# Two transformer blocks on one core: the gate's dense steps moved into the HGRN stage, and half the stick-breaking heads' values multiplied as whole float32 numbers

## The chip, the cores and the metric

The kernel runs on one core of a Trainium2 chip. The metric is device time in microseconds (us) for one launch, the median of three runs. The profile is one more execution, taken with the hardware profiler. Engines are named as in the profile: PE (matrix multiplies; PEld are its weight loads), DVE (vector), ACT (scalar and activation), POOL, and SP, which here only issues DMA transfers, in order.

## What is computed

Two blocks over 1024 tokens of width 1024, all in float32. Only the first block's mixing half is touched. There, one normed input `u` is multiplied by `w_in`, and the product is cut into four parts for HGRN (`hq`, `hf`, `hi` and the gate `hg`, 512 columns each) and three for stick-breaking attention (`sq`, `sk`, `sv`, 8 heads of 64):

```
o_hg = rmsnorm(hgrn2_mix(hq, hf, hi, lb)) * silu(hg)
z     = q.k * scale                              # causal, per head
rem   = cumsum_from_the_right(log(1 - sigmoid(z))) without its own term
a     = sigmoid(z) * exp(rem)
o_sb  = a @ v                                    # then rmsnorm
mix   = concat([o_hg, o_sb]) @ w_out
```

HGRN is a gated recurrence with 4 heads of 128. What follows (output projection, feed-forward, the whole second block) is the same in both kernels.

## The kernel before, in words

**Dense products.** A float32 product is made of rounded parts: every operand is split into a high part and a rest (`split`, line 215: a cast at L218, a subtraction at L224), and `mm3` (L300 to L302) issues three single-pass matmuls, high times high, high times rest, rest times high. A weight unit is 1024 columns by 128 rows of `w_in`. `a_steps` takes one unit for 128 output columns (48 matmuls), `b_steps` four units for 512 columns (8 steps of 24 matmuls). `Weights` loads units in the order in which `register` lists them, two raw loads and four split units at a time. Below, "dense matmul" always means one of L300 to L302.

**HGRN stage** (`mix1`). Each HGRN head is a chain of 12 steps (`hgrn_steps`): `diag`, seven levels `lev` (matmuls at L746, and on DVE and POOL the updates on which the next level depends), `kt`, `ds` and two `out`. `merge` deals these steps out among the dense steps of the list `main`.

**Stick-breaking stage** (`sb`). For a head and each of 8 strips of 128 queries, `score` multiplies q by k (L968, L969, a mask at L971), takes two sigmoids (ACT, L972, L973), a running product from the right (DVE, L975) and a product (DVE, L977). `pv_steps` then goes by pairs of strips: PE transposes the weights (L869), ACT copies them out as a high part (L872), DVE makes the rest (L873), and four matmuls of 256 or 128 columns multiply them by `vs`, which holds high and rest of v side by side in 128 columns (L882, L886, L888). The two halves are added at the end (ACT copy L892, DVE add L983). `after_pair` transposes and squares what two heads gave (L992, L996) and stores it to `osbT`. Ten such groups make a head.

The dense steps that `mix1` returns (`rest`) are dealt out among these steps. `load` of a head pair waits, by the third entry of its step, until the dense steps of that pair's q and k were recorded: q and k go through DRAM (store `ev_T`, L687; load L836, L839).

**The order.** A scheduler orders the recorded steps; stick-breaking steps have a priority 300 ahead of the dense ones (`AHEAD`). The order on each engine is then fixed when the kernel is built, and each engine works in that order.

**After it** `out1` multiplies by `w_out`, in two groups for each 128 tokens: one on the HGRN part, one on the stick-breaking part, which is read back from `osbT` (L1032).

Of the kernel before, what the change touches and what calls it, by code (L numbers as in the profile page):

```python
# [8 lines left out]
F32 = mybir.dt.float32  # L9
F32R = mybir.dt.float32r  # L10
# [8 lines left out]
P = 128  # L19
D = 1024  # L20
T = 1024
NT = T // P
# [174 lines left out]
class Kernel:  # L197
# [161 lines left out]
    def register(self):  # L359
        U = self.U = {}  # L360
        U["hi"] = self.b_units("w_in", 1024)
        pair = [("sq", 2048), ("sk", 2560)]
        for h in range(4):
            U["hq", h] = self.a_units("w_in", h * P, 1)
            U["hf", h] = self.a_units("w_in", 512 + h * P, 1)
            if h in (1, 2):

                U[pair[h - 1][0], 0] = self.a_units("w_in", pair[h - 1][1], 1)
        U["sv"] = self.b_units("w_in", 3072)
        for j in range(1, 4):  # L370
            for n, c0 in pair:
                U[n, j] = self.a_units("w_in", c0 + j * P, 1)
        U["hg"] = self.b_units("w_in", 1536)
        U["out"] = [self.b_units("w_out", c * 512, kind=("w", "xxxy")[c]) for c in range(2)]
        self.ffn_units(0, "w_gate_up", "w_gate_up", FF, "w_down", ("pg", "ple_gate", "ple_proj"))
        U["z0"] = self.b_units("w_in_2", 0, 416)
        U["dq"] = self.b_units("w_in_2", 416)
        U["dk"] = self.b_units("w_in_2", 928)
        U["dv"] = self.b_units("w_in_2", 1440)
        U["om"] = [self.b_units("w_out_2", c * 512, nk=4) for c in range(2)]  # L380
        U["od"] = [self.b_units("w_out_2", c * 512, k0=4, nk=4) for c in range(2)]
        self.ffn_units(1, "w_gate_2", "w_up_2", 0, "w_down_2", ("pg2", "w_ple_gate_2", "w_ple_proj_2"))
# [65 lines left out]
    def build(self):  # L448
        nc, A = self.nc, self.A
        self.constp = self.pool("const")  # L450
        self.smallp = self.pool("small", 4)
        self.junkp = self.pool("junk", 1)
        self.W = Weights(self, RAWS)
        self.W.open_raw("raw", RAWS, self.ctx)
        self.W.open("w", 4, self.ctx)
        self.psp = self.pool("psum", 1, space=PSUM)
        dram = self.pool("scratch", 1, space=DRAM)
        dt = lambda name, shape: dram.tile(shape, F32, tag=name, name=name)
        self.S = {n: dt(n, s) for n, s in dict(
            hgg=[T, 512], ohg=[T, 512], osbT=[512, T], h1=[T, D], h2=[T, D],  # L460
            rm=[4, 2, T], dv=[T, 512], omT=[512, T], od=[T, 512], h3=[T, D], act=[FF, T], bias8=[4, 1152], skew=[4, P * 1152]).items()}
        for n, sh in dict(qk=[96, 16, 2, T], vm=[T, 8, P], sq=[8, P, T], sk=[8, P, T], sv=[T, 8, P], dq=[8, P, T], dk=[8, P, T]).items():
            self.S[n] = dram.tile(sh, F32, tag=n, name=n)

        self.register()
        self.constants()
        self.block1()
# [175 lines left out]
    def mix1(self):  # L643
        nc, S, U = self.nc, self.S, self.U
        st = nc.sync.dma_start
        with ExitStack() as c:
# [41 lines left out]
                return f  # L688

            def ev_sv(ps, i):  # L690
                t = tmp.tile([P, 8, 2, 64], F32R, tag="hl", name="stage")
                self.split(t[:, :, 0, :], t[:, :, 1, :], ps.rearrange("p (h d) -> p h d", h=8), "act", "dve")
                st(out=S["sv"][i * P:(i + 1) * P], in_=t.rearrange("p h a d -> p h (a d)").bitcast(F32))

            def ev_gate(ps, i):
                s = tmp.tile([P, 512], F32, tag="s", name="sg")
# [4 lines left out]
            def head(h):  # L701
                return self.a_steps(U["hq", h][0], ev_q(h)) + self.a_steps(U["hf", h][0], ev_f(h))

            def pair(j):
                return (self.a_steps(U["sq", j][0], ev_T(S["sq"], j))
                        + self.a_steps(U["sk", j][0], ev_T(S["sk"], j)))

            first = head(0)
            p0 = pair(0)
            main = head(1) + p0[:8] + head(2) + p0[8:] + head(3) + self.b_steps(U["sv"], self.u_of, ev_sv) + pair(1)  # L710
            side = []
            for h in range(4):
                side += self.hgrn_steps(h, H[h])
            self.run(first + side[0:2])
            self.merge(side[2:], main, AHEAD["hg"], BY["hg"])
        return pair(2) + pair(3) + self.b_steps(U["hg"], self.u_of, ev_gate)

    def hgrn_steps(self, h, X):
        nc, S = self.nc, self.S
# [130 lines left out]
        first = 384 if ext == 640 else min(512, ext)  # L850
        return [(0, first)] + ([(first, ext - first)] if ext > first else [])

    def pv_steps(self, X, h, put):

        nc = self.nc
        out = {}
        for I in range(NT // 2):
            L = []
            for jp in range(I + 1):
                def f(I=I, jp=jp):  # L860
                    ps = self.ps("tr")
                    a0, a1 = X["a", 2 * I], X["a", 2 * I + 1]
                    j0, j1 = 2 * jp, 2 * jp + 1
                    if jp < I:
                        blocks = [(a0, j0), (a1, j0), (a0, j1), (a1, j1)]
                    else:
                        blocks = [(a0, j0), (a1, j0), (a1, j1)]
                    for n, (a, j) in enumerate(blocks):
                        nc.tensor.transpose(ps[:, n * P:(n + 1) * P], a[:, j * P:(j + 1) * P], self.ident)  # L869
                    w = len(blocks) * P  # L870
                    at = self.atp.tile([P, 2, 512], F32R, tag="at", name="at")
                    nc.scalar.copy(at[:, 0, 0:w], ps[:, 0:w])  # L872
                    nc.vector.tensor_tensor(at[:, 1, 0:w], ps[:, 0:w], at[:, 0, 0:w].bitcast(F32), ALU.subtract)  # L873
                    X["at", I, jp] = at

                def g(I=I, jp=jp):
                    if jp == 0:
                        X["pv"] = self.ps("pv")
                    pv, at, vs = X["pv"], X.pop(("at", I, jp)), X["v"]
                    j0, j1 = 2 * jp, 2 * jp + 1  # L880
                    for hl in range(2):
                        nc.tensor.matmul(pv[:, 0:256], vs[:, j0, :], at[:, hl, 0:256],  # L882
                                         start=jp == 0 and hl == 0, stop=False)
# [11 lines left out]
            out[I] = L  # L895
        return out

    def attention_steps(self, heads, load, score, make_put, after_pair, order, need=lambda h: 0):

        steps = []  # L900
        queue = []
# [11 lines left out]
        steps.append((0.1, prep(0)))  # L913
        prev = []
        for h in range(heads):
            L = self.pv_steps(X[h], h, make_put(X))
            left = list(range(NT // 2))
            for n, i in enumerate(order):
                if n == 2 and h + 1 < heads:
# [19 lines left out]
    def sb(self, rest):  # L939
        nc, S, U, A = self.nc, self.S, self.U, self.A  # L940
        self.banks = {"d": [0, 1], "z": [2, 3, 4], "tr": [5, 6], "pv": [7]}
        with ExitStack() as c:
# [8 lines left out]

            def load(h, X):
                X[h]["q"], X[h]["k"] = self.load_stack(S["sq"][h], S["sk"][h])
                X[h]["v"] = self.load_v(S["sv"], h)
                if h % 2 == 0:
                    X[h]["o"] = X[h + 1]["o"] = op.tile([P, T], F32, tag="o", name="sb_o")

# [22 lines left out]
            def make_put(X):  # L980
                def put(h, I, pv, t):
                    r = (h % 2) * 64
                    nc.vector.tensor_tensor(X[h]["o"][r:r + 64, I * 256:(I + 1) * 256], pv[0:64, 0:256], t, ALU.add)  # L983
                return put

# [12 lines left out]
                nc.scalar.activation(o, o, AF.Copy, scale=self.cols[:, COL_SB + j:COL_SB + j + 1])  # L998
                nc.sync.dma_start(out=S["osbT"][j * P:(j + 1) * P, :], in_=o)

            side = self.attention_steps(8, load, score, make_put, after_pair, ORDER["sb"], lambda h: max(0, h // 2 - 1) * 16)
            self.merge(side, rest, AHEAD["sb"], BY["sb"])


# [971 lines left out]
```

## Time and profile before

| | |
|---|---|
| runs | 2895.56, 2894.29, 2891.99 us; median 2894.29 |
| profiled execution | 2897.28 us, of which the span of its instructions is 2895.5 us |
| PE busy | 2777.6 us, 96% of the span |
| DVE busy | 1756.3 us, 61% |
| ACT busy | 1163.4 us, 40% |
| POOL busy | 712.3 us, 25% |
| granted PE clock | 0.991 of full speed on the mean |

Busy times are unions: what overlaps is counted once, and a matmul counts until its last result is out, so that a PE that is busy all the time need not be at its peak. All stages of both blocks are in these shares; the stage of interest lies between 62 and 600 us. Windows below are us from the start of the span.

### The profile page before, as it was taken

What the parts mean: (1) busy time and instruction counts of PE and PEld (TensorE: products, weight loads), DVE (VectorE), ACT (ScalarE), POOL (GpSimd) and SP (SyncE); (2) the same over time, 40 slices, a digit from 0 to 9 for tenths busy, and PEclk for the clock granted to TensorE, in tenths of its full rate; (3) what the DMA queues carried; (4) which work ended last, traced back from release to release, by engine and by line L of the source; (5) the groups of instructions that cost most, each with busy time, mean ns of one, the idle gap of its engine ahead of it and who ended that gap; (6) DMA issues with size and microseconds to landing.
All of it is one profiled execution on the core that took longest, in us unless ns stands there. A gap on an engine that the chain in (4) does not pass through costs nothing. (4 is left out here: it accounts for less than half of the span.)

```text
span 2895.5 us, 37271 instructions
## 1 busy us (share of the span) xinstructions
PE 2777.6 (96%) x13699; PEld 2281.7 (79%) x13699; DVE 1756.3 (61%) x3132; ACT 1163.4 (40%) x2237; POOL 712.3 (25%) x608
## 2 busy tenths in 40 slices
PE   8989998988999999999999999989999999999999
PEld 6878767776888888887788788767778888788887
DVE  4444598768444334667478775777875555556661
ACT  4211376745333334223246455656543333311131
POOL 1222100035433332223124000020243343222211
PEclk9989999999999999999999999999999999999999
DMA  4221645252322224332126855753422222343211
GB/s 134 73 71 65 175 124 135 93 183 73 95 87 84 83 78 165 102 104 91 65 102 178 217 151 175 203 131 76 139 73 81 80 88 87 118 166 104 77 65 46
DMA packets 277942, 321.36 MB, mean 111 GB/s; under 512 B 14646, under 2 KB 207194, under 8 KB 276222
## 3 DMA queue, kind: packets, MB, share of 16 engines
q1 hardware_dynamic: 277758, 318.97, 36.5%
q8 instruction: 108, 1.77, 0.3%
q14 instruction: 76, 0.62, 0.1%
HBM read 228.69 MB, written 92.59 MB: 111 GB/s over the span
## 5 line engine op out<-in xcount | busy, mean ns | idle before, releaser
L1249 PE MATMUL bank<-q,w 128*128 128x512 f32 x3696 | 846.6, 391 | 5.9 <-DVE q L1132 1.4
L1249 PEld LDWEIGHTS bank<-q,w 128*128 128x128 f32 x3696 | 693.3, 188 | 157.6 <-ACT s L1186 2.1
L218 ACT CAST w<-raw 128x1024 fp32r<-128x1024 f32 (+2 forms) x246 | 236.8, 971 | 495.9 <-DVE y L1315 185.9
L224 DVE TENSOR_TENSOR w<-raw,w 128x1024 fp32r<-128x1024 f32 (+2 forms) x242 | 311.7, 1297 | 128.1 <-ACT w L218 121.7
L1315 DVE TENSOR_TENSOR y<-y,bank 128x512 f32<-128x512 f32 x336 | 227.0, 686 | 162.1 <-PE bank L302 158.3
L300 PE MATMUL bank<-w,act 128*128 128x512 f32 x704 | 274.7, 390 | 2.7 <-DVE o L1231 2.7
L302 PE MATMUL bank<-w,act 128*128 128x512 f32 x704 | 274.7, 391 | 1.5 <-POOL act L224 1.5
L300 PE MATMUL bank<-w,u 128*128 128x512 f32 (+1 forms) x672 | 272.0, 405 | 3.1 <-DVE dn L1574 1.4
L301 PE MATMUL bank<-w,act 128*128 128x512 f32 x704 | 274.5, 390 | 0.0
L301 PE MATMUL bank<-w,u 128*128 128x512 f32 (+1 forms) x672 | 266.4, 396 | 3.3 <-POOL w L224 2.2
L302 PE MATMUL bank<-w,u 128*128 128x512 f32 (+1 forms) x672 | 265.9, 396 | 1.1 <-DVE u L296 1.1
L224 POOL TENSOR_TENSOR act<-act_raw,act 128x1024 fp32r<-128x1024 f32 x40 | 103.6, 2609 | 300.9 <-ACT act L218 300.9
L1186 ACT COPY s<-bank 128x512 f32<-128x512 f32 x132 | 77.4, 588 | 202.6 <-PE bank L1249 202.5
L300 PEld LDWEIGHTS bank<-w,act 128*128 128x128 f32 x704 | 132.6, 188 | 30.7 <-DVE o L1231 3.1
L302 PEld LDWEIGHTS bank<-w,act 128*128 128x128 f32 x704 | 132.5, 188 | 30.0 <-POOL act L224 2.2
L301 PEld LDWEIGHTS bank<-w,act 128*128 128x128 f32 x704 | 132.4, 188 | 27.2
L300 PEld LDWEIGHTS bank<-w,u 128*128 128x128 f32 x672 | 127.3, 189 | 26.6 <-ACT u L293 2.4
L301 PEld LDWEIGHTS bank<-w,u 128*128 128x128 f32 x672 | 127.2, 189 | 26.8 <-POOL w L224 3.1
L302 PEld LDWEIGHTS bank<-w,u 128*128 128x128 f32 x672 | 127.0, 189 | 26.2 <-DVE u L296 1.7
L224 DVE TENSOR_TENSOR w<-s,w 128x1024 fp32r<-128x1024 f32 x44 | 54.4, 1236 | 139.9 <-ACT w L218 139.9
L873 DVE TENSOR_TENSOR at<-bank,at 128x512 fp32r<-128x512 f32 (+1 forms) x160 | 99.8, 630 | 42.8 <-ACT at L872 41.6
L140 POOL TENSOR_TENSOR s<-raw 128x512 f32<-128x512 f32 x44 | 59.9, 1362 | 218.3 <-DVE w L224 137.4
(361 smaller groups left out, 5208.9 us busy)
## 6 DMA issues: line engine op xcount, KB each, us to landing
raw<-in_w_gate_up_dram SPq DMA_DIRECT2D x44, 512.0 KB
act<-o SPq DMA_DIRECT2D x88, 256.0 KB
raw<-in_w_down_dram SPq DMA_DIRECT2D x44, 512.0 KB
act_raw<-act SPq DMA_DIRECT2D x44, 512.0 KB
raw<-in_w_in_dram SPq DMA_DIRECT2D x40, 512.0 KB
qk<-qkT SPq DMA_DIRECT2D x32, 384.0 KB
raw<-in_w_gate_dram SPq DMA_DIRECT2D x22, 512.0 KB
raw<-in_w_up_dram SPq DMA_DIRECT2D x22, 512.0 KB
```

What stands on the lines that cost most here:

```text
L140: pool(x[:, HI], r2[:, LO], r2[:, HI], ALU.add)
L218: nc.scalar.copy(hi, src)
L224: e.tensor_tensor(lo, src, hi.bitcast(F32), ALU.subtract)
L300: mm(ps, lh, rh, start=start, stop=False)
L301: mm(ps, lh, rl, start=False, stop=False)
L302: mm(ps, ll, rh, start=False, stop=stop)
L873: nc.vector.tensor_tensor(at[:, 1, 0:w], ps[:, 0:w], at[:, 0, 0:w].bitcast(F32), ALU.subtract)
L1186: nc.scalar.copy(t, src)
L1249: nc.tensor.matmul(ps, w[:, a, o], (uh, ul)[b][:, k, :], start=bool(first) and n_mm == 0, stop=n_mm == 11, skip_group_check=True)
L1315: nc.vector.tensor_tensor(y, y, ps, ALU.add)
```

## The change

1. `register` and `mix1`: the gate's dense steps (`hg`, 8 steps of 24 matmuls) leave `rest` and become the last of the HGRN stage's `main`. In `main` the q and k products of stick-breaking pairs 0 and 1 now stand whole between the HGRN heads. `rest` keeps pairs 2 and 3.
2. Odd stick-breaking heads (1, 3, 5, 7): the weights are copied out of the transpose as whole float32 numbers, with no rest made on DVE. v is kept whole, 64 columns wide, in a DRAM tensor of its own (`sw`). Two float32 matmuls take the place of four single-pass ones; each is two instructions on PE. The result lies in 64 rows, and one ACT copy takes the place of a copy and a DVE add.
3. `ev_sv` splits only the even heads' half of v, and copies the odd half; it issues three stores for each 128 tokens where there was one.

```diff
         for h in range(4):
             U["hq", h] = self.a_units("w_in", h * P, 1)
             U["hf", h] = self.a_units("w_in", 512 + h * P, 1)
             if h in (1, 2):
 
-                U[pair[h - 1][0], 0] = self.a_units("w_in", pair[h - 1][1], 1)
+                pair_units(h - 1)
         U["sv"] = self.b_units("w_in", 3072)
-        for j in range(1, 4):
-            for n, c0 in pair:
-                U[n, j] = self.a_units("w_in", c0 + j * P, 1)
         U["hg"] = self.b_units("w_in", 1536)
+        pair_units(2)
+        pair_units(3)
...
             def ev_sv(ps, i):
-                t = tmp.tile([P, 8, 2, 64], F32R, tag="hl", name="stage")
-                self.split(t[:, :, 0, :], t[:, :, 1, :], ps.rearrange("p (h d) -> p h d", h=8), "act", "dve")
-                st(out=S["sv"][i * P:(i + 1) * P], in_=t.rearrange("p h a d -> p h (a d)").bitcast(F32))
+
+                t = tmp.tile([P, 3, 4, 64], F32R, tag="hl", name="stage")
+                v = ps.rearrange("p (h two d) -> p h two d", two=2, d=64)
+                w = t[:, 2].bitcast(F32)
+                self.split(t[:, 0], t[:, 1], v[:, :, 0], "act", "dve")
+                nc.scalar.copy(w, v[:, :, 1])
+                for a in range(2):
+                    st(out=S["sv"][i * P:(i + 1) * P, :, a * 64:(a + 1) * 64], in_=t[:, a].bitcast(F32))
+                st(out=S["sw"][:, :, i, :].rearrange("h p d -> p h d"), in_=w)
...
             first = head(0)
-            p0 = pair(0)
-            main = head(1) + p0[:8] + head(2) + p0[8:] + head(3) + self.b_steps(U["sv"], self.u_of, ev_sv) + pair(1)
+            main = (head(1) + pair(0) + head(2) + pair(1) + head(3) + self.b_steps(U["sv"], self.u_of, ev_sv)
+                    + self.b_steps(U["hg"], self.u_of, ev_gate))
...
-        return pair(2) + pair(3) + self.b_steps(U["hg"], self.u_of, ev_gate)
+        return pair(2) + pair(3)
...
+                    X["at", I, jp] = at
+                    if whole:
+                        nc.scalar.copy(at[:, 0, 0:w].bitcast(F32), ps[:, 0:w])
+                        return
...
+                    if whole:
+                        at = at[:, 0].bitcast(F32)
+                        o, n = (0, 256) if jp < I else (128, 128)
+                        nc.tensor.matmul(pv[0:64, 0:256], vs[:, j0, :], at[:, 0:256], start=jp == 0, stop=False)
+                        nc.tensor.matmul(pv[0:64, o:256], vs[:, j1, :], at[:, 256:256 + n], start=False, stop=jp == I)
+                        if jp == I:
+                            put(h, I, pv, None)
+                        return
...
+                    if t is None:
+                        nc.scalar.copy(X[h]["o"][r:r + 64, I * 256:(I + 1) * 256], pv[0:64, 0:256])
+                        return
...
-            side = self.attention_steps(8, load, score, make_put, after_pair, ORDER["sb"], lambda h: max(0, h // 2 - 1) * 16)
+            side = self.attention_steps(8, load, score, make_put, after_pair, ORDER["sb"], lambda h: max(0, h // 2 - 1) * 16, (1, 3, 5, 7))
```

**Where the dense matmuls now stand on PE.** Counted in the built order, among the steps of the HGRN heads and of the stick-breaking heads:

| dense matmuls on PE | before | now |
|---|---|---|
| up to the first score of head 0 | 968 | 1141 |
| within heads 0 to 3 | | 94 |
| in one block, after pair 1's last transposes and ahead of head 4's first score | 0 | 78 |
| within heads 4 and 5 | | 25 |
| after pair 2's last transposes and ahead of head 6's first score | 0 | 6 |
| within heads 6 and 7 | | 0 |
| from head 0's first score to pair 3's last transposes, in all | 322 | 203 |
| behind pair 3's last transposes, ahead of `out1` | 54 | 0 |

Three places in that order, on PE. In the names, `u` is the normed input, `w` a weight unit, `hk` and `hg_qp` a HGRN head's k and its growing q, `sb_o` a pair's output, `k` and `q` a stick-breaking head's, `oT` the operand of `out1`.

First place: the seven levels of HGRN head 1. Before, dense matmuls stood between the first three, and the last four stood in a row:

```order
L302 MATMUL bank_1237<-u_114,w 128x512
L746 MATMUL bank_1290<-hg_qp,hk 120x64 x8
L746 MATMUL bank_1329<-hg_qp,hk 112x64 x8
L746 MATMUL bank_1355<-hg_qp,hk 96x64 x8
L746 MATMUL bank_1391<-hg_qp,hk 64x64 x8
L779 MATMUL bank_1424<-ident,hk 128x128 x4
```

Now:

```order
L302 MATMUL bank_1197<-u_115,w 128x512
L756 MATMUL bank_1255<-hg_qp,hk 127x64 x8
L756 MATMUL bank_1290<-hg_qp,hk 126x64 x8
L756 MATMUL bank_1322<-hg_qp,hk 124x64 x8
L756 MATMUL bank_1368<-hg_qp,hk 120x64 x8
L756 MATMUL bank_1408<-hg_qp,hk 112x64 x8
L756 MATMUL bank_1451<-hg_qp,hk 96x64 x8
L756 MATMUL bank_1487<-hg_qp,hk 64x64 x8
L789 MATMUL bank_1520<-ident,hk 128x128 x4
```

All seven levels now stand with nothing between them.

Second place: the start of head 6 (its k is `k_3995` before, `k_4138` now; `w_3662` is a unit of the gate, `w_2627` pair 3's k unit). Before:

```order
L300 MATMUL bank1_3697<-w_3662,u0_113 128x512
L301 MATMUL bank1_3697<-w_3662,u0_113 128x512
L302 MATMUL bank1_3697<-w_3662,u0_113 128x512
L869 MATMUL bank5_4233<-ident_95,be_4060 128x128
L869 MATMUL bank5_4233<-ident_95,be_4097 128x128 x2
L968 MATMUL bank2_4225<-k_3995,q_3993 128x128
```

Now:

```order
L899 MATMUL bank7_4353<-at_4387,vs_3746 64x128
L1022 MATMUL bank6_4421<-ident_96,sb_o_3528 128x128 x4
L1022 MATMUL bank5_4434<-ident_96,sb_o_3528 128x128 x4
L300 MATMUL bank0_4101<-u1_115,w_2627 128x512
L301 MATMUL bank0_4101<-u1_115,w_2627 128x512
L302 MATMUL bank0_4101<-u1_115,w_2627 128x512
...
L995 MATMUL bank2_4309<-k_4138,q_4136 128x128
```

The last six dense matmuls of pair 3's k now stand behind the last work of heads 4 and 5 and directly ahead of the first score that reads that k; before, pair 3's k was complete 84 rows earlier.

Third place: the end of the stage. Before:

```order
L302 MATMUL bank0_4811<-w_3662,u1_114 128x512
L288 MATMUL bank7_5096<-ident_95,o_hg_5050 128x128 x4
L300 MATMUL bank5_5134<-w_4920,oT_5070 128x512
L301 MATMUL bank5_5134<-w_4920,oT_5070 128x512
L302 MATMUL bank5_5134<-w_4920,oT_5070 128x512
```

Now:

```order
L1022 MATMUL bank6_4831<-ident_96,sb_o_4143 128x128 x4
L1022 MATMUL bank5_4844<-ident_96,sb_o_4143 128x128 x4
L288 MATMUL bank7_4969<-ident_96,o_hg_4923 128x128 x4
L300 MATMUL bank0_5008<-w_4066,oT_4943 128x512
L288 MATMUL bank6_4976<-ident_96,o_hg_4946 128x128 x4
L300 MATMUL bank5_5007<-w_3162,oT_4943 128x512
```

The gate's last 54 matmuls no longer stand there, and the first dense matmul of `out1` (`w_4066`, the third unit of `w_out`) is one of the group that reads the stick-breaking part.

## Rows read from the trace of the kernel before

**Rows 1.** Windows of the span: length, busy us of each engine, granted clock, DMA.
```profile
core 0: us, PE busy (x) PEld busy (x) DVE busy (x) ACT busy (x) POOL busy (x), PEclk, DMA share, GB/s
62.00:162.00 100.00, 97.53 (x549) 81.03 (x547) 38.39 (x55) 23.11 (x36) 26.32 (x25) 1.00 0.21 65
162.00:190.00 28.00, 19.15 (x128) 17.73 (x127) 11.44 (x19) 4.14 (x6) 8.01 (x5) 0.70 0.00 1
190.00:340.50 150.50, 149.27 (x849) 127.92 (x847) 63.77 (x85) 32.78 (x49) 32.08 (x32) 1.00 0.40 120
340.50:450.20 109.70, 99.24 (x590) 76.32 (x590) 102.01 (x135) 75.42 (x184) 3.48 (x35) 1.00 0.55 141
450.20:565.20 115.00, 105.13 (x631) 84.88 (x630) 96.72 (x124) 75.83 (x194) 2.48 (x25) 1.00 0.31 90
565.20:577.50 12.30, 12.30 (x57) 10.16 (x55) 5.79 (x16) 11.23 (x27) 2.92 (x2) 1.00 0.85 289
```

**Rows 2.** Groups by line on DVE, window 340.5:565.2 (busy us, mean ns | idle before).
```profile
L975 DVE TENSOR_TENSOR_SCAN om<-om,zeros 128x128 f32<-128x128 f32 (+3 forms) x64 | 86.2, 1350 | 11.0 <-ACT om L972 10.6
L873 DVE TENSOR_TENSOR at<-bank,at 128x512 fp32r<-128x512 f32 (+1 forms) x80 | 49.3, 625 | 7.9 <-ACT at L872 7.6
L977 DVE TENSOR_TENSOR be<-be,om 128x128 f32<-128x128 f32 (+3 forms) x64 | 48.1, 751 | 3.2 <-DVE om L975 0.5
L983 DVE TENSOR_TENSOR sb_o<-bank,ot 64x256 f32<-64x256 f32 x32 | 13.1, 411 | 2.4 <-ACT ot L892 1.9
L224 DVE TENSOR_TENSOR w<-raw,w 128x1024 fp32r<-128x1024 f32 x5 | 6.1, 1224 | 0.7 <-ACT w L218 0.7
L224 DVE TENSOR_TENSOR stage<-bank,stage 128x512 fp32r<-128x512 f32 x8 | 5.4, 673 | 0.0
L698 DVE TENSOR_TENSOR sg<-bank,sg 128x512 f32<-128x512 f32 x5 | 3.4, 685 | 0.7 <-ACT sg L697 0.7
```

**Rows 3.** Timeline of PE, HGRN head 1: start us, us, what [idle before].
```profile
164.46 1.86 PE L746 MATMUL bank<-hg_qp,hk 128*120 128x64 f32 x16 [0.56 <-DVE hg_qp L763]
168.25 1.76 PE L746 MATMUL bank<-hg_qp,hk 128*112 128x64 f32 x16 [1.93 <-DVE hg_qp L763]
...
181.15 1.97 PE L779 MATMUL bank<-ident,hk 128*128 128x128 f32 x8 [1.75 <-POOL hk L764]
```

**Rows 4.** Timeline of PE: a float32 product, and single-pass matmuls of 256 columns.
```profile
65.89 2.09 PE L533 MATMUL bank<-oh,tab 32*4 32x384 f32 x6
...
443.76 0.40 PE L886 MATMUL bank<-at,vs 128*128 128x256 f32 x2
444.00 0.34 PE L968 MATMUL bank<-k,q 128*128 128x384 f32 x1
```

**Rows 5.** Windows in the second block's attention, with little dense work beside it.
```profile
1860.00:1900.00 40.00, 31.62 (x177) 22.28 (x176) 31.52 (x115) 26.33 (x73) 0.00 (x0) 1.00 0.61 138
```

**Rows 6.** Timeline of SP, round trip of k through DRAM (start us, us to issue).
```profile
352.53 2.28 SPq L687 DMA_DIRECT2D sk<-stage  x3
354.90 0.91 SPq L110 DMA_DIRECT2D raw<-in_w_in_dram  x1
357.87 1.24 SPq L839 DMA_DIRECT2D k<-sk  x2
```

**Rows 7.** Timelines of SP and ACT: a load of 512 KB and its first reader.
```profile
305.98 3.20 SPq L110 DMA_DIRECT2D raw<-in_w_in_dram  x2
...
309.67 1.05 ACT L218 CAST w<-raw 128x1024 fp32r<-128x1024 f32 x1
```

**Rows 8.** Timelines of SP and PE at the end of the stage.
```profile
567.00 0.33 SPq L999 DMA_DIRECT2D osbT<-sb_o  x1
...
571.51 0.37 SPq L1032 DMA_DIRECT2D o_sb<-osbT  x1
...
580.37 0.50 PE L300 MATMUL bank<-w,oT 128*128 128x512 f32 x1 [2.24 <-ACT oT L293]
```

**Rows 9.** Group by line on PE, window 340.5:565.2.
```profile
L882 PE MATMUL bank<-at,vs 128*128 128x256 f32 x160 | 44.6, 326 | 15.7 <-DVE sb_o L983 10.0 <-DVE at L873 5.0 <-ACT be L973 0.4
```

More of the change, by code (lines that the diff above doesn't have):

```diff
@@ L362, in register, with pair_units @@
         pair = [("sq", 2048), ("sk", 2560)]
+        def pair_units(j):
+            for n, c0 in pair:
+                U[n, j] = self.a_units("w_in", c0 + j * P, 1)
         for h in range(4):
@@ L461, in build @@
             rm=[4, 2, T], dv=[T, 512], omT=[512, T], od=[T, 512], h3=[T, D], act=[FF, T], bias8=[4, 1152], skew=[4, P * 1152]).items()}
-        for n, sh in dict(qk=[96, 16, 2, T], vm=[T, 8, P], sq=[8, P, T], sk=[8, P, T], sv=[T, 8, P], dq=[8, P, T], dk=[8, P, T]).items():
+        for n, sh in dict(qk=[96, 16, 2, T], vm=[T, 8, P], sq=[8, P, T], sk=[8, P, T], sv=[T, 4, P], sw=[4, P, NT, 64], dq=[8, P, T], dk=[8, P, T]).items():
             self.S[n] = dram.tile(sh, F32, tag=n, name=n)
@@ L851, in pieces, with pv_steps @@
         return [(0, first)] + ([(first, ext - first)] if ext > first else [])
-    def pv_steps(self, X, h, put):
+    def pv_steps(self, X, h, put, whole=False):
         nc = self.nc
@@ L871, in f @@
                     at = self.atp.tile([P, 2, 512], F32R, tag="at", name="at")
+                    X["at", I, jp] = at
+                    if whole:
+                        nc.scalar.copy(at[:, 0, 0:w].bitcast(F32), ps[:, 0:w])
+                        return
                     nc.scalar.copy(at[:, 0, 0:w], ps[:, 0:w])
                     nc.vector.tensor_tensor(at[:, 1, 0:w], ps[:, 0:w], at[:, 0, 0:w].bitcast(F32), ALU.subtract)
-                    X["at", I, jp] = at
                 def g(I=I, jp=jp):
@@ L896, in pv_steps, with attention_steps @@
         return out
-    def attention_steps(self, heads, load, score, make_put, after_pair, order, need=lambda h: 0):
+    def attention_steps(self, heads, load, score, make_put, after_pair, order, need=lambda h: 0, whole=()):
         steps = []
@@ L915, in attention_steps @@
         for h in range(heads):
-            L = self.pv_steps(X[h], h, make_put(X))
+            L = self.pv_steps(X[h], h, make_put(X), h in whole)
             left = list(range(NT // 2))
@@ L953, in load @@
                 X[h]["q"], X[h]["k"] = self.load_stack(S["sq"][h], S["sk"][h])
-                X[h]["v"] = self.load_v(S["sv"], h)
+                if h % 2 == 0:
+                    X[h]["v"] = self.load_v(S["sv"], h // 2)
+                else:
+                    w = self.avp.tile([P, NT, P], F32R, tag="vs", name="vs").rearrange("p c v -> p (c v)")[:, 0:NT * 64]
+                    nc.sync.dma_start(out=w.bitcast(F32), in_=S["sw"][h // 2].rearrange("p c d -> p (c d)"))
+                    X[h]["v"] = w.bitcast(F32).rearrange("p (c d) -> p c d", d=64)
                 if h % 2 == 0:
```

## The prediction

> **What bounds the kernel now.** I read the windows first, to see which stage has room. In the HGRN stage there are two parts [rows 1]. From 190 to 340.5 us PE is busy for 149.3 of 150.5 us: dense work put in there makes it longer by its whole length. Between 162 and 190 us lies a hole, PE busy 19.2 of 28 us at a granted clock of 0.70: that is HGRN head 1, whose last four levels stand bare, each waiting for what DVE or POOL made from the level before [rows 3]. In the stick-breaking stage (340.5 to 565.2, 224.7 us) DVE is busy 102.0 of 109.7 us (93%) in the first half and 96.7 of 115 us in the second, PE 99.2 and 105.1: both are near full, and DVE carries the first half. Behind it, 54 matmuls of the gate fill the time in which the last pair's output goes through DRAM, and `out1` starts at 580.4 [rows 8]. Next I read what DVE does in the stage, by line, to price what goes [rows 2], then the order of the built programs, to see what is left beside what.
>
> **The sum** is made against the profiled execution, 2897.3 us; the median of the runs, 2894.3, is 3.0 us below it.
>
> *Gate moved, first score of head 0 later: +39.4.* 173 more dense matmuls now stand ahead of the first score. The gate's own run of 54 took 12.3 us in a window with nothing but three last transposes beside them [rows 1], 0.228 us each; 173 x 0.228 = 39.4. Nothing hides them: this stage's PE is full. Its eight evictions and stores lie beside PE work, on DVE 63.8 of 150.5 us busy there; they cost nothing as long as PE is the bound, and some 5 us of DVE if it were not. The three stores in place of one for v add 16 issues on SP; their first reader, head 0's v, stands behind the whole gate, some 40 us later. Zero, at worst the 16 issues at 0.33 us [rows 8], 5 us, if the gate's weight loads waited behind them on SP.
>
> *HGRN head 1, bare for seven levels: +6.9.* The four bare levels took 181.15 - 164.46 = 16.7 us, 4.2 each [rows 3]. Three more are bare now: 12.5 us. Their own matmuls (1.86 us each) were PE work before as well, so 12.5 - 5.6 = 6.9 us of idle time is new; the dense matmuls that covered them are counted above or behind. Below: no gain, since the chain can't be shorter than its levels, but 5 us if the first levels go faster. Above: PE at half clock doubles the 1.86 in each of the three, 12.5 us.
>
> *Stick-breaking stage: -2.0.* DVE's four groups sum to 196.7 us [rows 2]; with the 14.9 us of weight splits and evictions in the same rows they come to 211.6, which overlap to the 198.7 of the windows, a factor of 0.94. So a head costs 23.1 us of DVE; an odd head loses its rests and adds, (49.3 + 13.1)/8 x 0.94 = 7.3 us, and a pair is left with 38.9. By the new order the stage falls into five pieces:
> - heads 0 to 3, with 94 dense matmuls. Before, 102.0 us of DVE, of which 4.4 are head 4's first strips (10 of 36 blocks of the 15.8 us that L975 and L977 take in a head). 102.0 - 4.4 - 2 x 7.3 = 83.0; at the same 93% 89.3, and 4 us until pair 1's last product is out: 93.
> - the block of 78 dense matmuls. Pair 1 is done ahead of it and head 4 not begun, so DVE and ACT stand idle: 78 x 0.228 = 17.8.
> - heads 4 and 5 alone with 25 dense matmuls: 38.9 and some 4 us of evictions and splits. Nothing in this stage shows a pair alone. The nearest rows are the first half's 93% and the second block's attention, where DVE is busy 31.5 of 40 us, 79% [rows 5]; 42.9 at these two is 46 to 54. I take the middle, 0.85, since the new piece also fills and drains by itself: 51.
> - the gap ahead of head 6. Its k is made by the six matmuls that stand directly ahead (1.4 us), then goes through ACT and DVE (some 0.7 each, by DVE's row [rows 2]), two stores (1.1), DRAM (at most the 3.1 us from the last store's issue, 354.8, to the load that waited for it, 357.9), two load issues (1.2) [rows 6], and a landing (at most 3.7, from issue to first reader of as large a load [rows 7]): 11.9 us in which no engine has anything else but the last pair's squares. Below: 6, if the stores and loads land in 1.5 us each. Before, this k was ready long ahead of head 6.
> - heads 6 and 7 with no dense work: 38.9 at 0.85 and the last product, 49 (46 to 54).
>
> Together 222.7 against 224.7. DVE gives up 29 us in four odd heads and PE 119 dense matmuls, 27 us, yet the stage hardly shortens: what it loses in work it gives back in the block, in the gap and in pairs with nothing beside them.
>
> *Whole-number products: 0.* A float32 product of 384 columns took 2.09 us for six instructions, some 0.32 each, two to a product [rows 4]. At 256 columns that is 2 x 0.215 = 0.43 us, against two single-pass matmuls at 0.12 (443.76 to 444.00, two) = 0.24. An odd head has 16 products of 256 columns and 4 of 128: 7.7 us, against 4.3 before. PE does 13.7 us more in four heads. I cost it at nothing, because in heads 4 to 7 DVE and ACT set the pace and PE has dense matmuls taken away; without that cover it costs up to 13.7. ACT copies as before, and its new copy takes the place of the one at L892.
>
> *End of the stage: -2.2.* Before, `out1` began 15.2 us after the last transposes (565.2 to 580.4), behind 54 matmuls of the gate. Now its first matmul reads the stick-breaking part: store 1.8 us after the transposes, load 4.5 later (567.0, 571.5) [rows 8], at most 3.7 to land [rows 7], 2 for the split: 12.0. That is 3.2 earlier, less 1 for a clock that falls while PE waits. Between -6 (`w_out` is split ahead now and its waits go) and +4.
>
> Sum: 39.4 + 6.9 - 2.0 + 0 - 2.2 = +42.1. The profiled execution would take 2939.4, the median 3.0 less: **2936.4**.
>
> **Rivals.**
> *A (faster).* The stick-breaking stage falls to DVE's remaining work: q and k of pairs 2 and 3 come early enough that the pairs run into each other, and the block and the gap vanish. DVE's 198.7 - 29.2 = 169.5 us at 93% are 182, 42 less than before; with +46.3 ahead of it and 14 less behind (the gate's 54 matmuls gone, and the wait covered), 10 us faster, 2885. It decides wherever pair 1's and pair 2's ends overlap the next pair's start. For it: DVE's 93% in the first half. Against it: on PE, which works in order, both ends stand ahead of the next pair's first score. 0.06.
> *B (clock).* Heads 4 to 7 leave PE so idle that its clock falls to 1.2 GHz. A pair alone has 29 us of PE work: 18,432 score columns at 0.12 for 256, 8.6; products, 7.7 + 4.3; 80 transposes of 128 float32 columns at 0.107 [rows 4], 8.6. At half clock that is 58 to 60, more than DVE's 49: +11 for heads 6 and 7, and half that for 4 and 5: 2953. Against it: in the second block PE was granted full clock at 31.6 of 40 us busy [rows 5]; for it: the hole of head 1, at 19.2 of 28, had 0.70 [rows 1]. 0.15.
> The Trainium skill ("TensorE: Matmul & The Clock Gate", Part 4, PE-mode transpose) says that transposes do not engage the full clock as matmuls do, and a bare pair is rich in transposes; by that rule B would be the likeliest case. The trace so far speaks against it: the stage's own windows, with 36 transposes in each of eight heads, have a clock of 1.00 [rows 1].
> *C (passes on the path).* The odd heads' products set the pace after all, because the two transposed tiles (`at`) are held longer by each: +13.7, 2950. For it: PE waited 15.7 us on DVE and ACT ahead of these products [rows 9], so they sit at the end of a chain. 0.12.
> *D.* Pieces of both signs cancel to no change: 0.02.
>
> **How the numbers follow.** Forecast 0.65, A 0.06, B 0.15, C 0.12, D 0.02. The forecast's own bounds: the pairs at 93% (-8), the gap at 6 (-6), the end (-4) and head 1 (-2) give 2916 if all fall together; the pairs at 79% (+8), head 1 (+6), the end (+6) give 2956. Down to 2904 it takes in half of the way to A; up to 2962 B and C with a slow pair. A measurement of this kernel can tell some 0.2% (6 us) from no change. Faster by over that: 0.06, A. Within it: 0.03. Slower: 0.91.
>
> **What would show it.** In the changed kernel's profile: the first score of head 0 near 387 us; a hole at head 1 of some 37 us with a clock of 0.7 or less; a stretch of 18 us without any scan on DVE between heads 3 and 4, and one of 10 us in which PE, DVE and ACT all idle ahead of head 6; last transposes of pair 3 near 610. DVE busy some 30 us less in all, PE busy more by less than that. I am wrong if the span grows by less than 20 us, which means that the pairs overlap, or if the first score comes by 375.

## The result and the profile after

The changed kernel took 2944.28 us (median of 4 runs, 2940.67 to 2945.42) beside 2894.68 for the kernel before on the same chip: ratio 1.0170, 95% interval 1.0158 to 1.0182, slower by 49.6 us. 2936.4 was forecast, with a range from 2904 to 2962. The profiled execution took 2943.77 us (its span is 2941.6), 46.5 us more than the profiled execution before; the terms below are compared with that.

Section 1 of the profile page of the changed kernel, busy time by engine:

```profile
PE 2801.7 (95%) x13699; PEld 2292.9 (78%) x13699; DVE 1729.0 (59%) x3076; ACT 1163.3 (40%) x2243; POOL 698.7 (24%) x608
```

Before, PE had 2777.6 and DVE 1756.3: DVE has 27 us less, PE 24 more. The windows of the changed kernel, cut where the order of its program cuts it (columns as in [rows 1]):

```profile
157.00:200.00 43.00, 28.33 (x167) 26.86 (x166) 14.87 (x22) 4.12 (x6) 10.76 (x7) 0.60 0.00 0
200.00:389.60 189.60, 187.99 (x1021) 160.26 (x1019) 69.67 (x93) 39.48 (x65) 28.75 (x32) 1.00 0.41 109
389.60:494.40 104.80, 95.78 (x544) 69.70 (x545) 84.14 (x101) 74.27 (x182) 3.14 (x32) 1.00 0.43 116
494.40:511.70 17.30, 17.30 (x78) 14.28 (x77) 4.53 (x5) 6.77 (x19) 0.00 (x0) 1.00 0.79 201
511.70:560.60 48.90, 42.71 (x251) 30.18 (x250) 39.05 (x47) 33.62 (x79) 1.58 (x16) 1.00 0.27 84
560.60:575.00 14.40, 1.39 (x7) 0.78 (x5) 1.92 (x2) 4.71 (x17) 0.00 (x0) 0.63 0.88 228
575.00:623.40 48.40, 40.76 (x224) 28.84 (x224) 41.98 (x49) 35.76 (x82) 1.18 (x12) 0.93 0.15 44
623.40:635.05 11.65, 0.91 (x4) 0.71 (x4) 6.27 (x18) 7.99 (x25) 2.48 (x2) 0.61 0.77 260
635.05:757.40 122.35, 111.66 (x506) 91.01 (x506) 87.34 (x161) 58.66 (x119) 57.68 (x34) 0.94 0.39 125
```

From the top: the hole at HGRN head 1; HGRN with the gate, PE busy 188.0 of 189.6 us; heads 0 to 3; the block of 78 dense matmuls, with DVE busy 4.5 of 17.3 us; heads 4 and 5; the gap ahead of head 6, with PE busy 1.4 of 14.4 us; heads 6 and 7; the wait for `out1`; and `out1` up to its last transposes. All the pieces that the prediction drew are there. What they measured:

| piece | before | after | change | forecast |
|---|---|---|---|---|
| first score of head 0 at | 340.6 | 389.6 | +49.0 | +46.3 |
| stick-breaking stage | 224.7 | 233.8 | +9.1 | -2.0 |
| heads 0 to 3 | | 104.8 | | 93 |
| block | | 17.3 | | 17.8 |
| heads 4 and 5 | | 48.9 | | 51 |
| gap | | 14.4 | | 11.9 |
| heads 6 and 7 | | 48.4 | | 49 |
| last transposes to `out1` | 15.2 | 11.65 | -3.5 | -2.2 |
| `out1` to its last transposes | 127.7 | 122.35 | -5.3 | 0 |
| all behind that, with what a launch has outside its span | | | -2.8 | 0 |
| sum | | | +46.5 | +42.1 |

So the sum came out near the forecast partly by luck, because two errors of opposite sign stand in it: heads 0 to 3 took 11.8 us more, and the end gave 9.4 us more than priced. The stage's costliest lines (groups by line on DVE and PE, window 389.6:623.4), which answer to [rows 2, 9]:

```profile
L1002 DVE TENSOR_TENSOR_SCAN om<-om,zeros 128x640 f32<-128x640 f32 (+5 forms) x64 | 85.6, 1346 | 23.5 <-ACT om L999 23.5
L1004 DVE TENSOR_TENSOR be<-be,om 128x640 f32<-128x640 f32 (+5 forms) x64 | 47.7, 747 | 3.0 <-ACT om L999 0.5
L888 DVE TENSOR_TENSOR at<-bank,at 128x512 fp32r<-128x512 f32 (+1 forms) x40 | 24.5, 616 | 0.0
...
L898 PE MATMUL bank<-at,vs 128*64 128x256 f32 x80 | 25.4, 399 | 1.4 <-DVE sb_o L1013 0.7 <-ACT sb_o L1011 0.4 <-ACT at L885 0.3
...
L899 PE MATMUL bank<-at,vs 128*64 128x256 f32 (+1 forms) x80 | 20.6, 339 | 0.0
```

The rests (`at`) fell from 80 to 40 instructions and from 49.3 to 24.5 us, as priced; the odd heads' products are 160 instructions on two lines.

### The profile page after: what moved, and what is told of

The parts are those of the page before. It is cut to its first block, busy times and chain, and to the rows that moved or that the text cites. A ratio compares the mean times of both kernels' runs of the same rounds, so it can differ in the third digit from the quotient of the medians.

```text
span 2941.6 us, 37269 instructions
## 1 busy us (share of the span) xinstructions
PE 2801.7 (95%) x13699; PEld 2292.9 (78%) x13699; DVE 1729.0 (59%) x3076; ACT 1163.3 (40%) x2243; POOL 698.7 (24%) x608
## 5 line engine op out<-in xcount | busy, mean ns | idle before, releaser
L300 PE MATMUL bank<-u,w 128*128 128x512 f32 x256 | 102.7, 402 | 0.4 <-DVE stage L224 0.4
```

Of the source, the lines that this page charges most:

```text
L300: mm(ps, lh, rh, start=start, stop=False)
```

## Experiments

The theory at the start: the order of the dense steps costs what the prediction says, and the whole-number products are free. The rivals were C (they are on the path) and that the stick-breaking pieces have other limits than those named. Each ratio is against the kernel before, in runs on the same chip.

**1. The two halves of the change, each alone.** The order without the products: `ev_sv`, `load` and the list of whole heads as before (only the last is shown).

```diff
-            side = self.attention_steps(8, ..., lambda h: max(0, h // 2 - 1) * 16, (1, 3, 5, 7))
+            side = self.attention_steps(8, ..., lambda h: max(0, h // 2 - 1) * 16)
```

> The new order of the dense steps without the whole-number products (every head's tile is split and its v stored as before). Theory (the order costs, the products are free): first score at 389 us as in the changed kernel; heads 0 to 3 within 3 us of 104.8, since DVE gets back 14.6 us of work but PE was the fuller engine there; heads 4 and 5 and heads 6 and 7 each some 7 us longer than 48.9 and 48.3, since a pair gets back two heads' worth of 7.3 us in one odd head and is bound by DVE: 2955 us, between 2945 and 2962. Rival C (the four-pass products are on the path): 13.7 us of PE go and nothing is lost: 2931.

2934.91 us, ratio 1.0142 (1.0127 to 1.0158): nearer to rival C's 2931 than to the theory's 2955. The products without the order: `register` (not shown), `main` and the returned steps as before.

```diff
+            p0 = pair(0)
+            main = head(1) + p0[:8] + head(2) + p0[8:] + head(3) + self.b_steps(U["sv"], self.u_of, ev_sv) + pair(1)
...
+        return pair(2) + pair(3) + self.b_steps(U["hg"], self.u_of, ev_gate)
```

> The whole-number products on the order of the kernel before. Theory: DVE gives up 29 us in the stick-breaking stage but PE takes 13.7 us more, 204 + 14 = 218 of its 224.7 us, so PE becomes the bound and the stage stays within 6 us: 2889 to 2900 us, no change to speak of. Rival C (products on the path in full): 2908. Rival A's half (DVE alone is the bound): stage 15 us or more shorter, 2880.

2904.07 us, ratio 1.0037 (1.0023 to 1.0051): slower, by 10 us, and between the theory's range and C's 2908. The theory falls in its second half. The order costs 41 us, the products 8 (1.0170 less 1.0142) or 10, and the two add up to the change within the runs' spread. What the products do on the order of before is seen in that run's window of the whole stage:

```profile
340.40:576.60 236.20, 223.83 (x1213) 158.98 (x1214) 171.22 (x202) 152.85 (x380) 5.90 (x60) 1.00 0.40 107
```

DVE fell from 198.7 to 171.2 us and PE rose from 204.4 to 223.8 of the stage [rows 1]; the stage went with PE, 224.7 to 236.2, and PE is now busy 95% of it. (Of PE's 19.4 us more, the sum of the products has 13.7; the rest was not traced to its source.) On the order of the change the products' effect lies elsewhere. Windows of the run with the order alone, in the same five pieces:

```profile
388.40:498.60 110.20, 95.77 (x565) 76.16 (x566) 101.44 (x132) 76.83 (x185) 3.17 (x32) 0.97 0.44 120
498.60:508.60 10.00, 9.38 (x42) 7.39 (x40) 1.11 (x2) 4.74 (x16) 0.00 (x0) 1.00 0.98 225
508.60:562.70 54.10, 44.26 (x270) 34.20 (x270) 49.27 (x65) 37.02 (x88) 1.58 (x16) 1.00 0.40 120
562.70:568.20 5.50, 0.02 (x1) 0.05 (x1) 0.00 (x0) 2.40 (x9) 0.00 (x0) 0.72 1.03 224
568.20:621.00 52.80, 39.77 (x224) 31.30 (x224) 49.47 (x63) 36.82 (x87) 1.19 (x12) 0.87 0.20 54
```

With two-pass products the heads are slower (110.2, 54.1 and 52.8 us against 104.8, 48.9 and 48.4), so the products did spare the pairs 15 us of DVE's pace. But the block is 10.0 and the gap 5.5 us, against 17.3 and 14.4: 16 us came back there. In heads 0 to 3 PE was busy 95.8 us in both runs, with longer products in the one and some 21 more dense matmuls (by the trace's records) in the other: what the longer products displaced went into the block. Within the stage the two sides cancel, 232.6 us against 233.8. Of the 6.3 us by which the two profiled spans differ, 1.2 lie ahead of the first score and 3.9 behind the stage, so on this order the price of 8 is not shown to be the products' time on PE.

**2. How much of it is the passes.** The odd heads' products in one pass, on either order.

```diff
-                        nc.scalar.copy(at[:, 0, 0:w].bitcast(F32), ps[:, 0:w])
+                        nc.scalar.copy(at[:, 0, 0:w], ps[:, 0:w])
...
-                        at = at[:, 0].bitcast(F32)
+                        at = at[:, 0]
...
-                    X[h]["v"] = w.bitcast(F32).rearrange("p (c d) -> p c d", d=64)
+                    X[h]["v"] = w.rearrange("p (c d) -> p c d", d=64)
```

> The run with the whole-number products on the order of before, with these products of the odd heads in one pass of rounded numbers in place of four of whole ones; the low parts are left out, all else stays (stores of v, loads, copies). Theory (what the whole-number products cost there is PE's time): PE's busy time in the stage falls from 223.8 us below the 204.4 of before, the stage follows it to 205 to 217 us: 2876 to 2888 us. Rival (the cost is in the new stores, loads or ACT copies): still 2898 or more.

2881.95 us, ratio 0.9954 (0.9941 to 0.9968). 22 us went with three passes out of four, and new stores, loads and copies stayed: the cost is PE's time. By the prediction's 7.7 us for an odd head, three quarters of four heads are 23 us: on this order nearly all of it is on the path.

> The changed kernel with the odd heads' products in one pass of rounded numbers; the low parts are left out, all else stays. On the order of before the same edit took 22 us off. Theory (passes are on the path where PE is full, as in heads 0 to 3 with 95.8 of 104.8 us, and half so in the pairs alone with 42.7 of 48.9 and 40.8 of 48.3): 8 us there and 2 to 4 in each later pair, 2928 to 2936. Passes on the path everywhere: 2920 to 2926. Passes hidden, as the prediction had it: 2941 or more.

2925.69 us, ratio 1.0108 (1.0092 to 1.0125), 18.6 us less than the change. That is more than my theory had, and its reason was wrong too, as the windows of this run show:

```profile
387.30:485.80 98.50, 87.62 (x529) 68.15 (x528) 87.12 (x104) 75.67 (x183) 3.14 (x32) 1.00 0.48 130
485.80:494.00 8.20, 8.20 (x37) 6.75 (x36) 0.69 (x1) 3.77 (x16) 0.00 (x0) 1.00 0.99 218
494.00:543.00 49.00, 41.24 (x252) 31.02 (x251) 42.47 (x51) 36.26 (x84) 1.57 (x16) 1.00 0.38 114
543.00:551.70 8.70, 0.00 (x0) 0.00 (x0) 0.00 (x0) 3.43 (x15) 0.00 (x0) 0.71 0.96 222
551.70:598.90 47.20, 35.84 (x204) 27.89 (x204) 40.79 (x48) 34.83 (x81) 1.18 (x12) 0.87 0.22 65
```

Heads 6 and 7, with no dense matmul in either run, take 47.2 us with one pass and 48.4 with four: there the passes are hidden but for 1.2 us, nearly as the prediction had it. Heads 4 and 5 take 49.0 and 48.9, but with some 21 more dense matmuls (by the trace's records) in the one-pass run, so that for them it is not shown. Heads 0 to 3 lose 6.3, the block 9.1 (37 matmuls in place of 78) and the gap 5.7.

**3. Why there is a block and a gap.** Pairs 2 and 3 in the HGRN stage, the gate's steps in the stick-breaking stage: 192 dense matmuls for 192. `register` follows, and `load` no longer waits for any of these steps (both not shown).

```diff
             main = (head(1) + pair(0) + head(2) + pair(1) + head(3) + self.b_steps(U["sv"], self.u_of, ev_sv)
-                    + self.b_steps(U["hg"], self.u_of, ev_gate))
+                    + pair(2) + pair(3))
...
-        return pair(2) + pair(3)
+        return self.b_steps(U["hg"], self.u_of, ev_gate)
```

> The changed kernel with the steps of pairs 2 and 3 in the HGRN stage and the gate's in the stick-breaking stage: 192 dense matmuls change places with 192, so every engine's work per stage is the same, and only the dependence goes (q and k of all heads are there at the start). Theory (block and gap come from late q and k): the block of 17.3 us and the gap of 14.4 us go, first score stays near 390, the stage falls from 233.7 to PE's 198 us at 95%, some 208: 2918 us, between 2912 and 2928. Rival L (the pairs are bound by their own chain whatever stands beside them, and the dense work comes on top): the stage shortens by the gap alone, 2930 to 2940.

2921.78 us, ratio 1.0093 (1.0078 to 1.0108); the stage took 202.0 us. Its windows, cut at pair 1's last transposes:

```profile
390.00:498.40 108.40, 100.04 (x567) 72.39 (x568) 86.22 (x105) 75.68 (x186) 3.54 (x36) 1.00 0.46 119
498.40:592.00 93.60, 86.69 (x498) 61.81 (x497) 74.48 (x87) 68.68 (x182) 2.36 (x24) 1.00 0.24 68
```

The stage shortened by 31.8 us, and block and gap had been 31.7: late q and k cause both. The dense work per stage did not stay quite the same: by the trace's records some 40 of the gate's matmuls stand in heads 6 and 7, where there had been none, and 35 behind the stage, where PE had waited for `out1`. Those among the heads cost nothing, 46 and 47 us a pair. The whole time fell by 22 only: behind `out1`'s start 8 us were lost again, the same 8 by which the change's end had been shorter. The same kernel without the whole-number products:

> The run with pairs 2 and 3 early, without the whole-number products. There PE was busy 186.7 and DVE 160.7 of the stage's 202 us. Without them PE has some 17 us less and DVE 29 us more, 190 us. Theory (the products cost PE time wherever PE is the fuller engine, and save DVE time wherever DVE is; here the two trade places): DVE at 93% makes the stage 204 us, 2922, between 2917 and 2927: the only order so far in which the products break even. Rival C in full (PE's time alone counts, DVE's never): 2906 to 2912.

2918.59 us, ratio 1.0076 (1.0060 to 1.0091), 3 us from the run above, inside the two runs' spread. PE was busy 181.7 us and DVE 192.4 of its stage's 206.4: where DVE is the fuller engine, the products break even in the whole time. (In the stage itself they gave 4.4 us, 206.4 against 202.0.)

Then the priority by which the dense steps of pairs 2 and 3 stand back.

```diff
-AHEAD = dict(hg=0, sb=300, mla=-20, diff=100)
+AHEAD = dict(hg=0, sb=100, mla=-20, diff=100)
```

> The changed kernel with the stick-breaking steps put ahead of the dense steps by 100 in place of 300, nothing else. In PE's order the block of 78 dense matmuls ahead of head 4 is spread (at most 18 stand together) and pair 3's k is made during head 5. Theory (the low priority of pairs 2 and 3's steps makes block and gap): both go, first score stays at 390, 2922 us, between 2914 and 2932. Rival L (dense work put between a pair's scores delays the pair by as much as the block did): only the gap goes, 2932 to 2942.

2935.62 us, ratio 1.0141 (1.0126 to 1.0156): the rival's figure. Window of heads 4 and 5 in this run:

```profile
502.30:564.40 62.10, 56.42 (x309) 40.68 (x308) 43.73 (x52) 38.32 (x95) 1.57 (x16) 1.00 0.45 115
```

The block is gone and so is the gap (head 6 begins 0.7 us after pair 2's last transposes), but the dense matmuls lengthen this one pair from 48.9 to 62.1 us, with PE busy 91%, and heads 0 to 3 from 104.8 to 109.0. By the trace's records 84 dense matmuls stand in the pair where 26 had stood, and 58 at 0.228 us are 13.2 us, all that it grew by. The block is not an accident of the priority: those matmuls have to be done ahead of head 6 or head 4, and PE has no room there for all of them.

**4. What three more bare levels cost.** The gate's steps behind the merge, and pair 0 dealt as before (`register` follows, not shown), so that HGRN's order is the old one.

```diff
+            p0 = pair(0)
+            main = head(1) + p0[:8] + head(2) + p0[8:] + head(3) + self.b_steps(U["sv"], self.u_of, ev_sv) + pair(1)
...
             self.merge(side[2:], main, AHEAD["hg"], BY["hg"])
+            self.run(self.b_steps(U["hg"], self.u_of, ev_gate))
```

> The changed kernel with the gate's steps issued behind the HGRN stage's merge instead of in it, and pair 0's steps dealt as before. In PE's order HGRN is then as in the kernel before (four bare levels at head 1, 12 to 18 dense matmuls at the others) and 126 dense matmuls of the gate stand among head 0's scores. Theory (three more bare levels cost 11.4 us: the hole took 43.0 us for 17.0 us of work at full clock, 26 lost, against 28.0 for 13.4 before, 14.6 lost): last transposes of pair 1 at 481 in place of 494, 2933 us, between 2928 and 2937. Rival (what a hole gives back is lost again at other HGRN levels and among head 0's scores, as with the HGRN steps ahead by 300): 2940 to 2946.

2937.15 us, ratio 1.0144 (1.0128 to 1.0159): 7.1 us less than the change, at the edge of the theory's range; pair 1's last transposes came at 484.7, with ten more dense matmuls (2.3 us) left to the block. That is near the prediction's +6.9, but it does not rule out the 11.4 read from clock and windows: the two ratios are each good to some 4 us, and the edit also puts 126 dense matmuls among head 0's scores. In the hole itself some 10 us came back: from 162 to 191 us in this run PE is busy 20.2 of 29.0 us at 0.65, so that by the same reading 15.9 us are lost there in place of 26. Where the other 3 went was not traced. HGRN with a higher priority, so that 7 dense matmuls follow each bare level:

```diff
-AHEAD = dict(hg=0, sb=300, mla=-20, diff=100)
+AHEAD = dict(hg=300, sb=300, mla=-20, diff=100)
```

> The changed kernel with the HGRN steps put ahead of the dense steps by 300 in place of 0, nothing else. In PE's order each of head 1's seven levels then has 7 dense matmuls behind it in place of none, and 132 dense matmuls fewer stand ahead of the first score. Theory (the bare levels are idle time that dense work can fill): of the 43.0 us from 157 to 200, in which PE is busy 28.3 us at a granted clock of 0.60, 17 us are work at full clock; the other 26 us go, less what a block among the scores gives back: 2918 to 2926 us. Rival (the level chain of DVE and POOL, some 5 us a level, sets the pace in every head and 7 dense matmuls, 1.6 us, hide only that much of it): 11 us from head 1 and as much lost in other heads, 2935 to 2944.

2943.38 us, ratio 1.0165 (1.0151 to 1.0179), no change beside the changed kernel's 1.0170, and in the rival's range. The same edit of the kernel before:

> The same on the kernel before: HGRN steps ahead by 300 in place of 0. Its hole from 162 to 190 us has PE busy 19.2 of 28 us at 0.70, 13.4 us of work at full clock. Theory: up to 14.6 us can go, half of it kept: 2880 to 2888 us. Rival (the chain sets the pace): 2892 to 2900.

2904.80 us, ratio 1.0030 (1.0018 to 1.0042), slower, which neither the theory nor the rival had. The level matmuls' group, window 90:358, of the changed kernel, and then of it with HGRN ahead by 300:

```profile
L756 PE MATMUL bank<-hg_qp,hk 128*127 128x64 f32 (+6 forms) x448 | 55.4, 285 | 14.4 <-DVE hg_qp L773 9.4 <-POOL hk L774 4.6 <-DVE hg_qp L737 0.3
```

```profile
L756 PE MATMUL bank<-hg_qp,hk 128*127 128x64 f32 (+6 forms) x448 | 53.3, 260 | 11.2 <-DVE hg_qp L773 7.7 <-POOL hk L774 2.3 <-DVE hg_qp L737 1.1
```

The hole went: in that run's window from 150 to 190 us PE is busy at full clock.

```profile
150.00:190.00 40.00, 37.24 (x231) 30.84 (x230) 15.54 (x24) 7.21 (x10) 8.30 (x6) 1.00 0.21 62
```

But the levels still wait 11.2 us in all: seven dense matmuls, 1.6 us, are too short a cover, and the waits are now spread over many levels of all heads. The gain was gone by the first score of head 0: it came at 358.3 us, 31.3 earlier than in the change, and the 132 dense matmuls that no longer stand ahead of it are 30.1 of that at 0.228 us. So what the hole gave back was lost in the other HGRN heads. The same reckoning finds the 10 us that the kernel before lost with this edit: its first score came at 319.9 in place of 340.6 us, 20.7 earlier, but some 138 dense matmuls fewer (by the trace's records) should have made that 31.4. Its levels waited 13.8 us where 10.1 were waited before; how the rest divides among them is not shown.

**5. A version that beats both.** If 7 dense matmuls a level are too few, 12 may do. In the kernel before, a larger BY hands out fewer dense steps to each HGRN step: in PE's order head 1 then has two bare levels in place of four, and the other heads' levels 12 dense matmuls each for the most part.

```diff
-BY = dict(hg=1.05, sb=1.0, mla=0.75, diff=1.0)
+BY = dict(hg=1.2, sb=1.0, mla=0.75, diff=1.0)
```

> The kernel before with the HGRN merge's BY at 1.2 in place of 1.05, nothing else: head 1 has two bare levels in place of four, every level of the other heads 12 dense matmuls, and 79 dense matmuls fewer stand ahead of the first score. Theory (bare levels cost what they idle): half of the hole's 14.6 us goes, 2885 to 2891, faster than both kernels. Rival (as in the runs with HGRN ahead by 300: the dense matmuls among head 0's scores lose it again): 2894 to 2904.

2891.32 us, ratio 0.9982 (0.9973 to 0.9991), at the upper edge of the theory's range. The level matmuls' group, window 90:315, first of the kernel before and then at 1.2:

```profile
L746 PE MATMUL bank<-hg_qp,hk 128*127 128x64 f32 (+6 forms) x448 | 49.5, 266 | 10.1 <-POOL hk L764 5.8 <-DVE hg_qp L763 4.0 <-DVE hg_qp L727 0.3
```

```profile
L746 PE MATMUL bank<-hg_qp,hk 128*127 128x64 f32 (+6 forms) x448 | 47.7, 259 | 5.4 <-POOL hk L764 3.6 <-DVE hg_qp L763 1.4 <-DVE hg_qp L727 0.3
```

The levels' waits fell by 4.7 us and the kernel by some 5. With BY at 1.3:

> The kernel before with the HGRN merge's BY at 1.3: head 1 has one bare level in place of two at 1.2 and four at 1.05, and 84 dense matmuls in one run among head 0's scores. Theory (each bare level that is covered gives some 2.5 us, as two of them gave 5.5 at 1.2): 2886 to 2890 us, 2 to 3 below the run at 1.2. Rival (with one level left the hole is cheap already, and what stands among head 0's scores costs as much): 2890 to 2895.

2888.12 us, ratio 0.9977 (0.9967 to 0.9987). The intervals of the two overlap, so that 1.3 beats 1.2 is not shown; that either beats the kernel before, by 5 to 6 us, is.

## Why the prediction was right, and where it was not

**The gate, +39.4, and the bare levels, +6.9: right in what they name, the levels priced somewhat low.** The first score came 49.0 us later where 46.3 were forecast. Read from the windows, the hole lost 11.4 us more than before, so that some 38 are left for 173 dense matmuls; putting HGRN's order back gave 7.1 of the whole time. So the levels cost between 7 and 11 us, within the bounds of 5 and 12.5 that the prediction gave. The hole was 43.0 us long where 37 had been named. The bare levels are these on PE's timeline (start, us, what, idle before), the first, the fourth and the last of the seven, then the transposes of `hk`:

```profile
157.01 1.88 PE L756 MATMUL bank<-hg_qp,hk 128*127 128x64 f32 x16
...
171.94 3.43 PE L756 MATMUL bank<-hg_qp,hk 128*120 128x64 f32 x16 [1.99 <-DVE hg_qp L773]
...
187.96 1.97 PE L756 MATMUL bank<-hg_qp,hk 128*64 128x64 f32 x16 [2.29 <-POOL hk L774]
191.67 1.97 PE L789 MATMUL bank<-ident,hk 128*128 128x128 f32 x8 [1.75 <-POOL hk L774]
```

Seven levels took 34.7 us, 5.0 each, against the 4.2 of the four before [rows 3]: the middle ones ran for 3.4 us in place of 1.86. The window there shows why, a granted clock of 0.50, the 1.2 GHz level, after a first level without dense matmuls behind it:

```profile
162.00:190.00 28.00, 17.28 (x91) 16.24 (x90) 8.07 (x10) 0.00 (x0) 7.72 (x5) 0.50 0.00 1
```

The upper bound, 12.5, was for that.

**Heads 0 to 3, 93: mis-sized; 104.8 were measured.** This is the step that failed, and with it the term "whole-number products: 0". I took these heads at 83.0 us of DVE work at 93%, and argued the products' cover from heads 4 to 7, where it held. But two of the four odd heads stand in heads 0 to 3, and there PE is the fuller engine now, 95.8 of 104.8 us, DVE 84.1. With one pass these heads took 98.5 us, and some 24 dense matmuls more stood in them; less these, at 0.228 us, it is 93, the forecast's figure (an estimate). The rows for that were at hand: 99.2 of PE's 109.7 us in the first half before [rows 1], with the passes added and DVE's work taken away. The products' price itself was right. In the profile after, on PE's timeline (start, us, what; x2, two instructions to a product of 256 columns), one follows the next by 0.43 us:

```profile
608.32 0.59 PE L899 MATMUL bank<-at,vs 128*64 128x256 f32 x2
608.75 0.59 PE L898 MATMUL bank<-at,vs 128*64 128x256 f32 x2
```

The Trainium skill ("FP8 and Floating Point Precision", TensorE Precision Notes) has a true float32 product as four passes. The trace agrees: 0.43 us against 0.12 for a single pass [rows 4].

**Rival C: right that the products are on the path, and its price nearly; its reason not shown.** It gave 13.7 us and 2950, which is nearer to the measured 2944.28 than the forecast is. The products cost 10 us on the order of before and 8 on the new one, net of what DVE gains, and three of their four passes alone 22 and 18.6. No run tests the reason that C gave, transposed tiles held longer; what the runs show is PE's time, in the stretches where PE is the fuller engine. I had given it 0.12.

**The block and the pairs alone: right.** 17.3 against 17.8; 48.9 and 48.4 against 51 and 49.

**The gap, 11.9: mis-sized by its landing; 14.4.** SP's timeline (start, us to issue) in the gap:

```profile
563.49 1.23 SPq L691 DMA_DIRECT2D sk<-stage  x2
565.22 0.39 SPq L110 DMA_DIRECT2D raw<-in_w_out_dram  x1
566.68 2.56 SPq L849 DMA_DIRECT2D k<-sk  x4
```

and PE's (start, us, what, idle before) at its end:

```profile
575.04 0.48 PE L995 MATMUL bank<-k,q 128*128 128x128 f32 x1 [13.05 <-DMA k<-sk]
```

The stores and the wait for them went as reckoned; but the first score came 8.4 us after the first load's issue, where 1.2 us for two issues and 3.7 from issue to reader [rows 7] had been reckoned. Four loads of 512 KB were issued there, not two; at the window's 228 GB/s, with the DMA engines at 0.88, their 2 MB alone take some 9 us (an estimate; no run has fewer loads there).

**The end, -2.2: too small; -3.5, -5.3 and -2.8.** The first is inside the bounds given. The other two, `out1` and what follows, had been put at nothing. The run with pairs 2 and 3 early, with the gate back in the stick-breaking stage, lost 8 us behind `out1`'s start again; but the changed kernel with one pass, whose gate is still out of the way, lost 4.6 of them too. In all the runs what follows `out1`'s start is shorter where `out1` starts later: 2310 to 2315 us where it starts by 610, 2304 to 2309 where it starts after 626. Why was not tried, so the cause of these 8 us stays open.

**Rival A** fell with the block and the gap. **Rival B** fell too: the pairs alone had a granted clock of 1.00 and 0.93, hardly below the 2.4 GHz level. The Trainium skill ("TensorE: Matmul & The Clock Gate", Part 4, PE-mode transpose) has the full clock not engage for transposes; in these pairs, with 80 transposes each among scores and products, the trace does not show that.

## What to carry to other kernels

Price an instruction that grows on one engine piece by piece, in every stretch where it stands, against the engine that will be fullest there after the edit and not the one that is fullest now: relieving DVE by 27 us was worth nothing where PE stood at 90% beside it. Work that others need late, such as q and k of the last pairs, is better done early than work nobody waits for, such as the gate: equal amounts, 22 us apart here. A hole is worth what the chain behind it still waits with the cover that you can give it; count the waits of the whole group of instructions, not the hole.

## What the runs showed that I had not expected

Only a part of what the longer products cost lengthened the heads in which they stand (6.3 us in heads 0 to 3, four passes against one). More of it surfaced behind them, as 78 dense matmuls in a block in place of 37, and as a later k, 14.4 us of gap in place of 8.7. A hole of 43.0 us in which PE was at a granted clock of 0.60 could be filled for no gain that the runs can tell from nothing, with the levels' waits falling only from 14.4 to 11.2 us; covering only two of four bare levels in the kernel before, with 12 dense matmuls each, gave 5.
